# Expert outputs gated on leaving PSUM, split in two fp32r parts and summed by a 0/1 matrix, with w1 and w3 in separate blocks of 8 KB

## The chip, the cores and the metric

The kernel runs on one core of a Trainium2 chip. The metric is the device time of the whole kernel in microseconds (us), as the median of a few runs. The engines are named as in the profile: PE is TensorE's matrix product (PEld its weight load), DVE is VectorE, ACT is ScalarE, POOL is GpSimd, SP is SyncE, which here mostly issues DMAs.

## The reference, cut to what matters

Two transformer blocks run one after the other on 1024 tokens of 1024 numbers. The change touches only the mixture of experts of the first. It has 64 experts in 8 groups of 8. A token takes one group and in it two experts. Each expert is three matrices, w1 and w3 of 1024 x 256 and w2 of 256 x 1024, so 1 MiB each in fp32.

```python
g_sel = jnp.argmax(g_logits, axis=-1)
g_w = g_prob[tok, g_sel]
...
top_p, top_i = lax.top_k(e_prob, MOE_TOPK)
gates = g_w[:, None] * top_p / jnp.sum(top_p, axis=-1, keepdims=True)
expert_id = g_sel[:, None] * MOE_PER_GROUP + top_i
...
    hid = jax.nn.silu(xb @ w1[e]) * (xb @ w3[e])
    return hid @ w2[e]
...
ys = ys * slot_gate[:, None].astype(ys.dtype)
out = jnp.zeros((n_tok + 1, dm), ys.dtype).at[slot_tok].add(ys)[:n_tok]
```

## The kernel before

The program is three phases: a gated linear attention block, the mixture of experts (`phase_moe`), and the second block. `phase_moe` keeps the tokens of a group together, at most 160 rows a group, and works on **pairs of experts**: 32 iterations (p = 0 to 31), four pairs to a group, each expert with 64 slots for its rows. The two experts of a pair share TensorE's array: one writes the PSUM rows 0 to 63, the other 64 to 127.

*One iteration on TensorE, in order.* `down_t` turns the hidden values of pair p-1 (two transposes into `mhd`, copied by VectorE to `hidT`, L1002). `slots_in` gathers the rows of pair p into slots, 32 bf16 products by a 0/1 matrix `Ms` (L1189, L1194), copied by ScalarE to `xT`. `rows_out(p - 2)` adds the outputs `my` of pair p-2 into the group's rows: a product by `MwT`, which holds each slot's gate at its token, of two halves of 512 columns for the first 128 tokens (L1220, into `Y0`) and of four quarters of 256 columns side by side for the other 32 (L1224, into `Y1`); each result leaves PSUM by an addition on VectorE, or by a copy for the first pair of a group (L1214, L1216). `hidden(p)` is eight contraction steps for two experts, w1 and w3 side by side as 512 columns (L986), fp32 in two passes; then ScalarE's silu (L990) and VectorE's product (L992). `turned` turns the gate matrix `Mw` of the pair to `MwT` (two transposes into `mwt`, one copy on ScalarE, L1205). `down(p - 1)` multiplies by w2 in two halves (L1014), the first copied to `my` by ScalarE, the second by VectorE (both L1016). `masks(p + 1)` builds the next `Ms` and `Mw` on VectorE (L1177 to L1180) ahead of that copy.

*PSUM.* The outputs of `down` and of `rows_out` share three buffers called `mpy`; `mh`, `mhd` and `mwt` have one each.

*The loads.* All weights of the experts are read on SP's queue in the order of the program: `load_13` (L918 to L925) reads w1 and w3 of an expert into columns 0 to 255 and 256 to 511 of one tile of 128 x 8 x 512, so each row of eight steps lands in pieces of 256 numbers, 1 KB; `load_2` (L926 to L928) reads w2 in pieces of 8 KB. There are seven slots (`Slots`): iteration p issues w1 and w3 of experts 2p+7 and 2p+8 (from p = 12 on one fewer ahead) and w2 of two experts. The DMAs carry their completions on eight semaphore lanes, used in turn by SP's loads and by ScalarE's stores of a group's rows (`y_d`, `write_group`, L1161 to L1166, after every fourth pair); a DMA waits for the last one on its lane.

Of the kernel before, what the change touches and what calls it, by code (L numbers as in the profile page):

```python
# [8 lines left out]
F32 = mybir.dt.float32  # L9
F32R = mybir.dt.float32r  # L10
# [3 lines left out]
ACT = mybir.ActivationFunctionType  # L14
ALU = mybir.AluOpType
# [55 lines left out]
class Slots:  # L71
# [24 lines left out]
    def w13(self, i):  # L96

        if i == 1:
            return self.raw.rearrange("p a (b c) -> p (a b) c", c=512)
        return self.tile(i, "w13", [128, 8, 512])  # L100

    def w2(self, i):
        return self.tile(i, "w2", [128, 2, D])
# [809 lines left out]
def expert_loads(k, w1, w3, w2):  # L913

    nc = k.nc

    def row(w, e):
        return w[e] if isinstance(e, int) else w[bass.ds(e, 1)].rearrange("o a b -> (o a) b")  # L918

    def load_13(e, w, parts=1, eng=(nc.sync, nc.sync)):  # L920
        n = 8 // parts
        for k0 in range(0, 8, n):
            for c, src in enumerate((w1, w3)):
                eng[c].dma_start(out=w[:, k0:k0 + n, c * 256:c * 256 + 256],  # L924
                                 in_=row(src, e).rearrange("(p k) f -> p k f", k=8)[:, k0:k0 + n, :])  # L925

    def load_2(e, w, eng=nc.sync):
        eng.dma_start(out=w, in_=row(w2, e).rearrange("(p k) d -> p k d", k=2))  # L928

    return load_13, load_2  # L930


def phase_moe(k, h2_d, x1_d, y_d, keep, slots, load_13, load_2, w0):

    tc, nc = k.tc, k.nc
    V, S, G = nc.vector, nc.scalar, nc.gpsimd
    with ExitStack() as ctx:
# [22 lines left out]

        get_2(1)

        for name, n in (("my", D), ("MwT", GCAP)):
            sp.tile([128, n], F32, name=name)
        xa, xb = slots.xg, sp.tile([64, D], F32, name="xg1")
        i128 = sp.tile([128, 128], F32, name="mi128")
        G.iota(i128, pattern=[[1, 128]], base=0, channel_multiplier=0, allow_small_or_imprecise_dtypes=True)
# [12 lines left out]
        def hidden(xT, *ws):  # L980

            n = 64 * len(ws)
            h = php.tile([128, 512], F32, name="mh", tag="mh")
            for kk in range(8):
                for c, w in enumerate(ws):
                    nc.tensor.matmul(h[c * 64:c * 64 + 64, :], xT[:, kk, c * 64:c * 64 + 64], w[:, kk, :],  # L986
                                     start=(kk == 0), stop=(kk == 7), skip_group_check=True)

            hid = sp.tile([128, 2, 128], F32, name="hid")
            S.activation(out=hid[0:n].rearrange("s k p -> s p k"), in_=h[0:n, 0:256].rearrange("s (p k) -> s p k", k=2),  # L990
                         func=ACT.Silu)
# [12 lines left out]

        def down(hT, *ws):

            n = 64 * len(ws)
            y = sp.tile([128, D], F32, name="my")
            for half, copy in ((0, S.copy), (1, V.tensor_copy)):
                cs = slice(half * 512, half * 512 + 512)  # L1010
                ps = pyp.tile([128, 512], F32, name="mpy", tag="mpy")
                for kk in range(2):
                    for c, w in enumerate(ws):
                        nc.tensor.matmul(ps[c * 64:c * 64 + 64, :], hT[:, kk, c * 64:c * 64 + 64], w[:, kk, cs],  # L1014
                                         start=(kk == 0), stop=(kk == 1), skip_group_check=True)
# [17 lines left out]
        with tc.If(most > GCAP), ExitStack() as over:  # L1033
# [83 lines left out]

            V.tensor_scalar(out=ox, in0=og[:, 0:NB], scalar1=float(FAR), scalar2=None, op0=ALU.add)
            wa, wb = slots.w13(6), slots.w2(6)
            x = ov.tile([64, D], F32, name="ox")  # L1120
            V.memset(x, 0.0)
            for j in range(NB):
                e = nc.sync.value_load(ebi[0:1, j:j + 1], min_val=0, max_val=63)
                load_13(e, wa)
                load_2(e, wb)
                gather(x, h2_d, ox[0:64, j:j + 1])
                xT = sp.tile([128, 8, 128], F32, name="xT")
                for half in range(2):
                    ps = ptp.tile([128, 4, 128], F32, name="mtr", tag="mtr")
                    for i in range(4):  # L1130
                        kk = half * 4 + i
                        k.transpose(ps[:, i, 0:64], x[:, kk * 128:(kk + 1) * 128])
                    S.copy(out=xT[:, half * 4:half * 4 + 4, 0:64], in_=ps[:, :, 0:64])
                y = list(down(down_t(hidden(xT, wa)), wb))[-1]
# [11 lines left out]
        Y0, Y1 = yp.tile([128, D], F32, name="Y0"), yp.tile([128, 256], F32, name="Y1")  # L1146

        def parts(eng=G, cuts=(slice(0, D),)):

# [12 lines left out]
        def write_group(g):  # L1162
            r = g * GCAP
            for cs in (slice(0, D),) if g < 7 else (slice(0, 512), slice(512, D)):
                S.dma_start(out=y_d[r:r + 128, cs], in_=Y0[:, cs])
            S.dma_start(out=y_d[r + 128:r + GCAP, :].rearrange("t (h c) -> h t c", h=4), in_=Y1)  # L1166

        def masks(p):

# [29 lines left out]
        def turned(w):  # L1199

            ps = phd.tile([128, GCAP], F32, name="mwt", tag="mwt")
            k.transpose(ps[:, 0:128], w[:, 0, :])
            k.transpose(ps[:, 128:GCAP], w[0:32, 1, :])
            wT = sp.tile([128, GCAP], F32, name="MwT", bufs=2)
            S.copy(out=wT, in_=ps)  # L1205
            return wT

        def rows_out(p, wT, y):

            first = p % 4 == 0  # L1210

            def into(out, ps, copy):
                if first:
                    copy(out, ps)  # L1214
                else:
                    V.tensor_tensor(out=out, in0=ps, in1=out, op=ALU.add)  # L1216
            for half in range(2):
                cs = slice(half * 512, half * 512 + 512)
                ps = pyp.tile([128, 512], F32, name="mpy", tag="mpy")
                nc.tensor.matmul(ps, wT[:, 0:128], y[:, cs], start=True, stop=True)  # L1220
                into(Y0[:, cs], ps, (S.copy, V.tensor_copy)[half])
            ps = pyp.tile([128, 256], F32, name="mpy1", tag="mpy")
# [15 lines left out]
        def pair(d, q):  # L1238
            return d.pop(2 * q), d.pop(2 * q + 1)
# [3 lines left out]
        for p in range(NP):  # L1243
            if p:
                hT = down_t(hid)
            xT = slots_in(m[0])
            if p > 1:
                rows_out(p - 2, wT.pop(p - 2), ys.pop(p - 2))
# [12 lines left out]
            if p:  # L1261
                d = down(hT, *pair(w2, p - 1))
# [1387 lines left out]
```

## Time and profile before

| | |
|---|---|
| median of three runs | 2372.03 us (2367.10 to 2373.81) |
| profiled execution | 2370.45 us |
| its span in the profile | 2368.5 us, granted clock 0.973 on the mean |
| PE busy over the span | 2235.8 us, 94% |
| DVE, ACT, POOL busy | 1376.2, 859.9, 569.1 us |
| bytes moved by DMA | 408.61 MB, 173 GB/s on the mean |

The profiled execution is one of its own, and the page's times lie within its span. An engine's busy time is a sum over stages that have different limits. The loop over pairs is the stretch from about 570 to 1080 us; read the rows below for that stretch and not for the whole.

### The profile page before, as it was taken

To read this page: it belongs to the slowest core of one execution; us is meant where nothing else is said; L and a number is where in the kernel's file an instruction comes from. 1 tells how busy PE (TensorE), PEld (TensorE's weight loads), DVE (VectorE), ACT (ScalarE), POOL (GpSimd) and SP (SyncE) were. 2 spreads that over 40 slices of the span, in tenths; PEclk is the share of its full clock that TensorE was granted. 3 is DMA by queue.
4 is the path that set the end of the run, shared out by engine and by line. 5 is a ranking of instruction groups with operands and counts; after the bars stand their busy time and mean duration, and the time that the engine had idled before them with its cause. 6 is when DMAs were issued, how large, how long until landed. Compare 5 with 4: busy or idle time off the path is not lost.

```text
span 2368.5 us, 31053 instructions
## 1 busy us (share of the span) xinstructions
PE 2235.8 (94%) x11879; PEld 1609.8 (68%) x11879; DVE 1376.2 (58%) x2378; ACT 859.9 (36%) x1610; POOL 569.1 (24%) x520
## 2 busy tenths in 40 slices
PE   8899999996999999998999999999979999999996
PEld 7778888873444444434766788777768888887884
DVE  4766524564443333325355524666588888878988
ACT  4342434311222222214443334424444444444443
POOL 3222223201111111005300100346443333310036
PEclk9999999996999999997999999999989999999999
DMA  5544211648999999997511022444432222227442
GB/s 175 180 123 140 90 33 31 241 179 302 382 395 384 378 374 397 389 395 209 144 39 30 10 43 58 147 99 134 160 98 81 81 81 84 84 91 293 132 138 80
DMA packets 325054, 408.61 MB, mean 173 GB/s; under 512 B 43016, under 2 KB 264312, under 8 KB 316704
## 3 DMA queue, kind: packets, MB, share of 16 engines
q1 hardware_dynamic: 312064, 368.23, 45.9%
q0 software_dynamic: 4944, 18.37, 2.7%
q10 hardware_dynamic: 7888, 19.93, 2.2%
q8 instruction: 96, 1.57, 0.3%
q14 instruction: 62, 0.51, 0.1%
HBM read 360.29 MB, written 46.19 MB: 172 GB/s over the span
## 4 chain that ended last, share of the span: by engine, by line
PE 57%; DVE 5%; DMA 5%; SPq 3%; issue 3%; POOL 2%; ACT 2%; POOLq 0%; DVEq 0%; ACTq 0%
PE mh L986 8%; PE pu L2208 5%; PE pu L2211 5%; PE pu L2210 5%; PE mpy L1014 4%; PE pj L1356 2%; PE pj L1354 2%; PE pj L1352 2%; SPq L924 2%; PE pu L2389 2%; PE mpy L1220 2%; PE pu L2390 2%; PE pu L2387 2%; DMA w<-in_moe_w_dram 2%; PE mtr L1189 1%
## 5 line engine op out<-in xcount | busy, mean ns | idle before, releaser
L986 PE MATMUL mh<-w,xT 128*64 128x512 f32 x880 | 233.4, 598 | 5.7 <-DMA w<-in_moe_w_dram 5.1
L136 POOL TENSOR_TENSOR whl<-wraw,whl 128x1024 fp32r<-128x1024 f32 x35 | 87.1, 2494 | 327.7 <-ACT whl L135 186.5
L986 PEld LDWEIGHTS mh<-w,xT 128*64 128x64 f32 x880 | 76.0, 137 | 123.7 <-issue 108.9
L992 DVE TENSOR_TENSOR hid<-hid,mh 128x256 f32<-128x256 f32 x32 | 13.5, 421 | 220.5 <-ACT hid L990 220.5
L1014 PE MATMUL mpy<-w,hidT 128*64 128x512 f32 x512 | 117.1, 599 | 0.0
L1159 POOL TENSOR_TENSOR xg<-xg,xp 32x1024 f32<-32x1024 f32 x7 | 20.3, 2904 | 372.1 <-ACT xp L1155 372.1
L309 PE MATMUL pj<-hT,whl 128*128 128x512 f32 x256 | 105.4, 412 | 0.7 <-ACT rT L447 0.7
L1356 PE MATMUL pj<-hT,whl 128*128 128x512 f32 x256 | 102.9, 402 | 0.5 <-POOL whl L136 0.5
L1354 PE MATMUL pj<-hT,whl 128*128 128x512 f32 x256 | 103.0, 402 | 0.0
L1352 PE MATMUL pj<-hT,whl 128*128 128x512 f32 x256 | 102.3, 400 | 0.0
L990 ACT ACTIVATE hid<-mh 128x256 f32<-128x256 f32 x32 | 19.8, 619 | 223.9 <-PE mh L986 223.9
L311 PE MATMUL pj<-hT,whl 128*128 128x512 f32 x256 | 100.7, 394 | 0.0
L310 PE MATMUL pj<-hT,whl 128*128 128x512 f32 x256 | 100.5, 393 | 0.0
L2096 POOL TENSOR_TENSOR gr<-wraw,gr 128x512 f32<-128x512 f32 x30 | 58.0, 1932 | 164.2 <-DVE wup L136 59.1
L258 PE MATMUL pj<-whl,hT 128*128 128x256 f32 x256 | 82.5, 322 | 0.6 <-ACT hT L135 0.4
L2217 DVE TENSOR_TENSOR fup<-pu,fup 128x512 f32<-128x512 f32 x100 | 68.6, 686 | 23.0 <-PE pu L2211 23.0
L2389 PE MATMUL pu<-wup 128*128 128x512 f32 x180 | 71.7, 398 | 6.6 <-DVE wup L136 6.6
L259 PE MATMUL pj<-whl,hT 128*128 128x256 f32 x256 | 74.5, 291 | 2.0 <-POOL whl L136 2.0
L260 PE MATMUL pj<-whl,hT 128*128 128x256 f32 x256 | 74.3, 290 | 0.0
L1014 PEld LDWEIGHTS mpy<-w,hidT 128*64 128x64 f32 x512 | 33.8, 136 | 56.1 <-issue 49.1
L504 DVE SCALAR_TENSOR_TENSOR oT<-oT,cv 128x512 f32<-128x512 f32 x84 | 70.5, 839 | 1.4
L2390 PE MATMUL pu<-wup 128*128 128x512 f32 x180 | 70.6, 392 | 0.0
(742 smaller groups left out, 6414.3 us busy)
## 6 DMA issues: line engine op xcount, KB each, us to landing
w<-in_moe_w_dram SPq DMA_DIRECT2D x164, 1024.0 KB
oT<-in_w_ada_dram SPq DMA_DIRECT2D x96, 256.0 KB
wraw<-in_w_up_dram SPq DMA_DIRECT2D x34, 512.0 KB
wraw<-in_moe_w_dram SPq DMA_DIRECT2D x16, 1024.0 KB
wraw<-in_gla_w_in_dram SPq DMA_DIRECT2D x24, 512.0 KB
wraw<-in_w_in_dram SPq DMA_DIRECT2D x22, 512.0 KB
act_d<-act SPq DMA_DIRECT2D x22, 512.0 KB
wraw<-in_w_down_dram SPq DMA_DIRECT2D x42, 256.0 KB
```

The lines of the kernel that those rows point to most:

```text
L309: nc.tensor.matmul(ps, w[:, 0, cs], hT[:, 0, kk, sl], start=(kk == 0), stop=False)
L311: nc.tensor.matmul(ps, w[:, 1, cs], hT[:, 0, kk, sl], start=False, stop=(kk == 7))
L986: nc.tensor.matmul(h[c * 64:c * 64 + 64, :], xT[:, kk, c * 64:c * 64 + 64], w[:, kk, :], start=(kk == 0), stop=(kk == 7), skip_group_check ...
L1014: nc.tensor.matmul(ps[c * 64:c * 64 + 64, :], hT[:, kk, c * 64:c * 64 + 64], w[:, kk, cs], start=(kk == 0), stop=(kk == 1), skip_group_che ...
L1352: nc.tensor.matmul(ps, w[:, 0, cs], hT[:, 0, kk, sl], start=(kk == 0), stop=False)
L1354: nc.tensor.matmul(ps, w[:, 0, cs], hT[:, 1, kk, sl], start=False, stop=False)
L1356: nc.tensor.matmul(ps, w[:, 1, cs], hT[:, 0, kk, sl], start=False, stop=(kk == 7))
L2208: nc.tensor.matmul(ps, w[:, 0, cs], hi[:, kk, :], start=(kk == 0 and q in (1, 6, 7, 5)), stop=False, skip_group_check=True)
L2210: nc.tensor.matmul(ps, w[:, 0, cs], lo[:, kk, :], start=False, stop=False, skip_group_check=True)
L2211: nc.tensor.matmul(ps, w[:, 1, cs], hi[:, kk, :], start=False, stop=(kk == 3), skip_group_check=True)
L2389: nc.tensor.matmul(ps, a[:, 0, ts], w[:, 1, :], start=False, stop=False, skip_group_check=True)
L2390: nc.tensor.matmul(ps, a[:, 1, ts], w[:, 0, :], start=False, stop=(kk == 10), skip_group_check=True)
```

## The change

Four things are edited, and the rest follows from them.

1. w1 and w3 go into two blocks of the tile (`w13` is now 128 x 2 x 8 x 256), so a row of one expert's matrix lands as one piece of 8 KB. `hidden` reads its 512 columns as two runs of 256, one from each block.
2. The gates move from the sum to the outputs: `turned` makes `MwT` a 0/1 matrix by a comparison on VectorE, and ScalarE sums its rows to `Mgate`, one gate per slot. `down` scales by it on leaving PSUM.
3. `my` has two fp32r parts: ScalarE writes the scaled output rounded, VectorE the scaled output less that. `rows_out` multiplies both by the 0/1 matrix and adds them in PSUM, with 512 columns each; `Y1` is 32 x 1024 now.
4. The software DMA queue's scratch is halved (8192 bytes).

Blocks beyond a group's 160 rows or an expert's 64 go through a branch of their own, which keeps plain copies (`down1`).

```diff
-        return self.tile(i, "w13", [128, 8, 512])
+        return self.tile(i, "w13", [128, 2, 8, 256])
...
-                eng[c].dma_start(out=w[:, k0:k0 + n, c * 256:c * 256 + 256],
+                eng[c].dma_start(out=w[:, c, k0:k0 + n, :],
...
-                    nc.tensor.matmul(h[c * 64:c * 64 + 64, :], xT[:, kk, c * 64:c * 64 + 64], w[:, kk, :],
-                                     start=(kk == 0), stop=(kk == 7), skip_group_check=True)
+                    nc.tensor.matmul(h[c * 64:c * 64 + 64, :].rearrange("s (a f) -> s a f", a=2),
+                                     xT[:, kk, c * 64:c * 64 + 64], w[:, :, kk, :], start=(kk == 0), stop=(kk == 7),
+                                     skip_group_check=True)
...
-        def down(hT, *ws):
+        def down(hT, gate, *ws):
...
-            y = sp.tile([128, D], F32, name="my")
-            for half, copy in ((0, S.copy), (1, V.tensor_copy)):
+            y = sp.tile([128, 2, D], F32R, name="my")
+            for half in range(2):
...
-                copy(y[0:n, cs], ps[0:n])
+                S.activation(out=y[0:n, 0, cs], in_=ps[0:n], func=ACT.Copy, scale=gate)
+                V.scalar_tensor_tensor(out=y[0:n, 1, cs], in0=ps[0:n], scalar=gate, in1=y[0:n, 0, cs].bitcast(F32),
+                                       op0=ALU.mult, op1=ALU.subtract)
...
-            wT = sp.tile([128, GCAP], F32, name="MwT", bufs=2)
-            S.copy(out=wT, in_=ps)
-            return wT
+            wT = sp.tile([128, GCAP], F32R, name="MwT", bufs=2)
+            gate = sp.tile([128, 1], F32, name="Mgate", bufs=2)
+            junk = sp.tile([128, GCAP], F32, name="Mj")
+            V.tensor_scalar(out=wT, in0=ps, scalar1=0.0, scalar2=None, op0=ALU.not_equal)
+            S.activation(out=junk, in_=ps, func=ACT.Copy, accum_out=gate)
+            return wT, gate
...
-            for half in range(2):
-                cs = slice(half * 512, half * 512 + 512)
-                ps = pyp.tile([128, 512], F32, name="mpy", tag="mpy")
-                nc.tensor.matmul(ps, wT[:, 0:128], y[:, cs], start=True, stop=True)
-                into(Y0[:, cs], ps, (S.copy, V.tensor_copy)[half])
-            ps = pyp.tile([128, 256], F32, name="mpy1", tag="mpy")
-            for i in range(4):
-                nc.tensor.matmul(ps[i * 32:i * 32 + 32], wT[:, 128:GCAP], y[:, i * 256:i * 256 + 256], start=True,
-                                 stop=True, skip_group_check=True)
-            into(Y1, ps, S.copy)
+            for Yn, n, r in ((Y0, 128, 0), (Y1, GCAP - 128, 128)):
+                for half in range(2):
+                    cs = slice(half * 512, half * 512 + 512)
+                    ps = pyp.tile([128, 512], F32, name="mpy", tag="mpy")[0:n]
+                    for i in range(2):
+                        nc.tensor.matmul(ps, wT[:, r:r + n], y[:, i, cs], start=(i == 0), stop=(i == 1))
+                    into(Yn[:, cs], ps, (S.copy, V.tensor_copy)[half])
...
-    nc = _bacc.Bacc("TRN2", target_bir_lowering=False, num_devices=1)
+    nc = _bacc.Bacc("TRN2", target_bir_lowering=False, num_devices=1, dynamic_dma_scratch_size=8192)
```

On TensorE, between the gathering of a pair's slots (L1194) and its hidden product (L986), there stood before:

```order
L1194 LDWEIGHTS xp_9277
L1194 MATMUL mtr<-Ms,xp_9277 128x128
L1220 MATMUL mpy<-my,MwT 128x512 x2
L1224 MATMUL mpy_10802<-my,MwT 32x256 x4
L986 MATMUL mh<-w_5_4720,xT 64x512
L986 MATMUL mh<-w_6_5046,xT 64x512
```

And in the changed program, at the same place of another pair:

```order
L1209 LDWEIGHTS xp_9276
L1209 MATMUL mtr<-Ms,xp_9276 128x128
L1240 MATMUL mpy<-my,MwT 128x512 x4
L1240 MATMUL mpy<-my,MwT 32x512 x4
L986 MATMUL mh<-wraw,xT 64x512
L986 MATMUL mh<-w_3_4708,xT 64x512
```

The sum is eight products in place of six, at the same place; what stands around it has not moved.

On VectorE, from the second half of a pair's masks (L1177) to the next pair's hidden product (L992), there stood before:

```order
L1177 TENSOR_SCALAR Ma<-mi_4703,cq 128x128 [waits DVE_49]
L1178 SCALAR_TENSOR_TENSOR Ms<-mi_4703,cq,Ma 128x128 [waits DVE_49]
L1179 TENSOR_SCALAR Mw<-mi_4703,cq,sgate 128x128
L1180 SCALAR_TENSOR_TENSOR Mw<-Ma,sgate,Mw 128x128 [waits DVE_49]
L1016 COPY my<-mpy 128x512 [waits PE_49]
L1002 COPY hidT<-mhd 128x256 [waits PE_49]
L1216 TENSOR_TENSOR Y_9278<-mpy,Y_9278 128x512 [waits PE_49] x2
L1216 TENSOR_TENSOR Y_9279<-mpy_10349,Y_9279 128x256 [waits PE_49]
L992 TENSOR_TENSOR hid<-hid,mh 128x256 [waits Activation_49]
```

And in the changed program, up to the comparison that now follows the hidden product (L1222):

```order
L1192 TENSOR_SCALAR Ma<-mi_4703,cq 128x128 [waits DVE_49]
L1193 SCALAR_TENSOR_TENSOR Ms<-mi_4703,cq,Ma 128x128 [waits DVE_49]
L1194 TENSOR_SCALAR Mw<-mi_4703,cq,sgate 128x128
L1195 SCALAR_TENSOR_TENSOR Mw<-Ma,sgate,Mw 128x128 [waits DVE_49]
L1018 SCALAR_TENSOR_TENSOR my<-mpy,Mgate,my 128x512 [waits Activation_49] x2
L1003 COPY hidT<-mhd 128x256 [waits PE_49]
L1234 TENSOR_TENSOR Y_9277<-mpy,Y_9277 128x512 [waits PE_49] x2
L1234 TENSOR_TENSOR Y_9278<-mpy,Y_9278 32x512 [waits PE_49] x2
L993 TENSOR_TENSOR hid<-hid,mh 128x256 [waits Activation_49]
L1222 TENSOR_SCALAR MwT<-mwt 128x160 [waits PE_49]
```

Two passes that wait for ScalarE stand where one copy waited for TensorE, and the comparison stands ahead of the next masks.

## Rows read from the trace of the kernel before

**Rows 1.** Windows: stretch; us; PE, PEld, DVE, ACT, POOL busy; PEclk; DMA share; GB/s

```profile
720.00:760.00 40.00, 40.00 (x256) 16.62 (x255) 15.30 (x33) 10.93 (x18) 6.96 (x4) 1.00 1.07 398
960.00:1000.00 40.00, 37.53 (x218) 17.80 (x216) 13.20 (x28) 9.86 (x16) 3.76 (x2) 1.00 1.05 393
```

**Rows 2.** Timeline of ScalarE: start us; us; instruction; idle before and its releaser

```profile
606.58 0.62 ACT L990 ACTIVATE hid<-mh 128x256 f32<-128x256 f32 x1 [6.65 <-PE mh L986]
...
839.67 0.62 ACT L990 ACTIVATE hid<-mh 128x256 f32<-128x256 f32 x1 [8.55 <-PE mh L986]
...
1067.31 0.62 ACT L990 ACTIVATE hid<-mh 128x256 f32<-128x256 f32 x1 [8.46 <-PE mh L986]
```

**Rows 3.** Waits, 560 to 1085 us: who waited for what; us, times, longest

```profile
PE mh L986 <- DMA w<-in_moe_w_dram: 5.1, 3, 2.5
...
PEld mh L986 <- DMA w<-in_moe_w_dram: 4.4, 2, 2.6
```

**Rows 4.** Waits of SP's queue, the same stretch and columns

```profile
SPq L928 <- DMA y_d<-Y: 10.4, 3, 9.1
```

**Rows 5.** Timeline of SP's queue, 839 to 841 us

```profile
839.44 1.41 SPq L928 DMA_DIRECT2D w<-in_moe_w_dram  x2
```

**Rows 6.** Windows, around pair 17's silu, columns as in rows 1

```profile
837.50:840.50 3.00, 3.00 (x16) 1.02 (x14) 0.18 (x1) 0.76 (x2) 0.00 (x0) 1.00 0.47 131
```

**Rows 7.** DMA packets: 732 to 736 us (w1, w3), then 857.3 to 861.3 (w2)

```profile
DMA packets 1539, 1.54 MB, mean 386 GB/s; under 512 B 32, under 2 KB 1539, under 8 KB 1539
...
DMA packets 235, 1.71 MB, mean 428 GB/s; under 512 B 20, under 2 KB 28, under 8 KB 28
```

**Rows 8.** Timeline of PE, one pair's sums and its hidden product

```profile
798.95 1.94 PE L1220 MATMUL mpy<-my,MwT 128*128 128x512 f32 x4
...
801.38 0.64 PE L986 MATMUL mh<-wraw,xT 128*64 128x512 f32 x1
...
807.87 0.59 PE L986 MATMUL mh<-wraw,xT 128*64 128x512 f32 x1
```

**Rows 9.** Timeline of PE, fp32r products of the attention phase

```profile
250.06 0.39 PE L309 MATMUL pj<-hT,whl 128*128 128x512 f32 x1
...
250.74 0.39 PE L309 MATMUL pj<-hT,whl 128*128 128x512 f32 x1
...
48.02 0.39 PE L327 MATMUL pj<-hT,walr 128*32 128x512 f32 x1
48.24 0.40 PE L326 MATMUL pj<-hT,walr 128*32 128x512 f32 x1
...
41.64 0.28 PE L260 MATMUL pj<-whl,hT 128*128 128x256 f32 x1
41.76 0.28 PE L258 MATMUL pj<-whl,hT 128*128 128x256 f32 x1
```

**Rows 10.** Groups by line and shape (count; busy us, mean ns; idle before)

```profile
L1016 DVE COPY my<-mpy 128x512 f32<-128x512 f32 x32 | 22.1, 691 | 13.5 <-PE mpy L1014 13.5
L1016 ACT COPY my<-mpy 128x512 f32<-128x512 f32 x32 | 18.7, 585 | 54.7 <-PE mpy L1014 30.9 <-issue 14.1 <-DVE Mw L1180 9.6
L1216 DVE TENSOR_TENSOR Y<-mpy,Y 128x512 f32<-128x512 f32 x48 | 33.2, 692 | 49.1 <-PE mpy L1220 49.1
L1002 DVE COPY hidT<-mhd 128x256 f32<-128x256 f32 x32 | 13.3, 415 | 3.5 <-PE mpy L1014 3.5
L1205 ACT COPY MwT<-mwt 128x160 f32<-128x160 f32 x32 | 10.7, 333 | 0.0
...
L1750 DVE SCALAR_TENSOR_TENSOR xbcT<-u,cw,xbcT 128x512 f32<-128x512 f32 x39 | 28.7, 804 | 0.0
```

**Rows 11.** Timeline of VectorE, the end of one pair's masks

```profile
796.31 0.35 DVE L1180 SCALAR_TENSOR_TENSOR Mw<-Ma,sgate,Mw 128x128 f32<-128x128 bf16 x1
797.03 0.69 DVE L1016 COPY my<-mpy 128x512 f32<-128x512 f32 x1 [0.37 <-PE mpy L1014]
```

More of the change, by code (lines that the diff above doesn't have):

```diff
@@ L98, in w13 @@
         if i == 1:
-            return self.raw.rearrange("p a (b c) -> p (a b) c", c=512)
-        return self.tile(i, "w13", [128, 8, 512])
+            return self.raw.rearrange("p (c x) (b f) -> p c (x b) f", c=2, f=256)
+        return self.tile(i, "w13", [128, 2, 8, 256])
     def w2(self, i):
@@ L961, in phase_moe @@
         get_2(1)
-        for name, n in (("my", D), ("MwT", GCAP)):
-            sp.tile([128, n], F32, name=name)
+        sp.tile([128, 2, D], F32R, name="my")
+        sp.tile([128, GCAP], F32R, name="MwT")
         xa, xb = slots.xg, sp.tile([64, D], F32, name="xg1")
@@ L1015, in down, with down1 @@
                                          start=(kk == 0), stop=(kk == 1), skip_group_check=True)
-                copy(y[0:n, cs], ps[0:n])
+                S.activation(out=y[0:n, 0, cs], in_=ps[0:n], func=ACT.Copy, scale=gate)
+                V.scalar_tensor_tensor(out=y[0:n, 1, cs], in0=ps[0:n], scalar=gate, in1=y[0:n, 0, cs].bitcast(F32),
+                                       op0=ALU.mult, op1=ALU.subtract)
                 yield y[0:n]
+        def down1(hT, w):
+            y = sp.tile([128, 2, D], F32R, name="my").rearrange("p a d -> p (a d)").bitcast(F32)[0:64, 0:D]
+            for half, copy in ((0, S.copy), (1, V.tensor_copy)):
+                cs = slice(half * 512, half * 512 + 512)
+                ps = pyp.tile([128, 512], F32, name="mpy", tag="mpy")
+                for kk in range(2):
+                    nc.tensor.matmul(ps[0:64, :], hT[:, kk, 0:64], w[:, kk, cs], start=(kk == 0), stop=(kk == 1),
+                                     skip_group_check=True)
+                copy(y[:, cs], ps[0:64])
+            return y
         NP = 32
@@ L1119, in phase_moe @@
             wa, wb = slots.w13(6), slots.w2(6)
-            x = ov.tile([64, D], F32, name="ox")
+            x = xb
             V.memset(x, 0.0)
@@ L1133, in phase_moe @@
                     S.copy(out=xT[:, half * 4:half * 4 + 4, 0:64], in_=ps[:, :, 0:64])
-                y = list(down(down_t(hidden(xT, wa)), wb))[-1]
+                y = down1(down_t(hidden(xT, wa)), wb)
                 xo = sp.tile([128, 8, 128], F32, name="oxa", tag="xT")[0:64].rearrange("p a b -> p (a b)")
@@ L1145, in phase_moe @@
         pb = yp.tile([96, D], BF16, name="xp1")
-        Y0, Y1 = yp.tile([128, D], F32, name="Y0"), yp.tile([128, 256], F32, name="Y1")
+        Y0, Y1 = yp.tile([128, D], F32, name="Y0"), yp.tile([GCAP - 128, D], F32, name="Y1")
         def parts(eng=G, cuts=(slice(0, D),)):
@@ L1165, in write_group @@
                 S.dma_start(out=y_d[r:r + 128, cs], in_=Y0[:, cs])
-            S.dma_start(out=y_d[r + 128:r + GCAP, :].rearrange("t (h c) -> h t c", h=4), in_=Y1)
+            S.dma_start(out=y_d[r + 128:r + GCAP, :], in_=Y1)
         def masks(p):
@@ L1216, in into @@
                     V.tensor_tensor(out=out, in0=ps, in1=out, op=ALU.add)
-            for half in range(2):
-                cs = slice(half * 512, half * 512 + 512)
-                ps = pyp.tile([128, 512], F32, name="mpy", tag="mpy")
-                nc.tensor.matmul(ps, wT[:, 0:128], y[:, cs], start=True, stop=True)
-                into(Y0[:, cs], ps, (S.copy, V.tensor_copy)[half])
-            ps = pyp.tile([128, 256], F32, name="mpy1", tag="mpy")
-            for i in range(4):
-                nc.tensor.matmul(ps[i * 32:i * 32 + 32], wT[:, 128:GCAP], y[:, i * 256:i * 256 + 256], start=True,
-                                 stop=True, skip_group_check=True)
-            into(Y1, ps, S.copy)
+            for Yn, n, r in ((Y0, 128, 0), (Y1, GCAP - 128, 128)):
+                for half in range(2):
+                    cs = slice(half * 512, half * 512 + 512)
+                    ps = pyp.tile([128, 512], F32, name="mpy", tag="mpy")[0:n]
+                    for i in range(2):
+                        nc.tensor.matmul(ps, wT[:, r:r + n], y[:, i, cs], start=(i == 0), stop=(i == 1))
+                    into(Yn[:, cs], ps, (S.copy, V.tensor_copy)[half])
             if p % 4 == 3:
@@ L1247, in phase_moe @@
             if p > 1:
-                rows_out(p - 2, wT.pop(p - 2), ys.pop(p - 2))
+                rows_out(p - 2, wT.pop(p - 2)[0], ys.pop(p - 2))
             if p % 4 == 3 and p // 4 + 1 < 8:
@@ L1261, in phase_moe @@
             if p:
-                d = down(hT, *pair(w2, p - 1))
+                d = down(hT, wT[p - 1][1], *pair(w2, p - 1))
                 ys[p - 1] = next(d)
@@ L1268, in phase_moe @@
                 get_2(*range(*e2[-2:]))
-        rows_out(NP - 2, wT.pop(NP - 2), ys.pop(NP - 2))
-        y = list(down(hT, *pair(w2, NP - 1)))[-1]
-        rows_out(NP - 1, wT.pop(NP - 1), y)
+        rows_out(NP - 2, wT.pop(NP - 2)[0], ys.pop(NP - 2))
+        rows, gate = wT.pop(NP - 1)
+        y = list(down(hT, gate, *pair(w2, NP - 1)))[-1]
+        rows_out(NP - 1, rows, y)
 def pipeline(make, n, every=1, front=False):
```

## The prediction

> **What bounds the kernel now.** I read the busy time by stretch first, because the change lies in one stage: the expert loop, from about 570 to 1080 us of 2368.5. There TensorE is busy for the whole of 720 to 760 us, and the DMA engines are at a share above 1 in the same stretch [rows 1]. Two resources are full at once, so the question is which of them sets each part of the stage.
>
> The silu that follows each pair's first product (L990) marks the pairs. From pair 2 to pair 17 it comes every (839.67 - 606.58) / 15 = 15.54 us, from pair 17 to pair 31 every (1067.31 - 839.67) / 14 = 16.26 us [rows 2]. The first part has TensorE without a gap: TensorE binds. In the second, TensorE falls to 37.53 of 40 us [rows 1] and it waits for weights, 5.1 + 4.4 us by name [rows 3]. The excess over the first pace is 227.64 - 14 x 15.54 = 10.1 us. So the weight loads bind the second part.
>
> Why only there? SP's queue issues the loads in order, and each also waits for the last transfer on its semaphore lane, on which group outputs (y_d) ride too. SP stood 9.1 us in one such wait [rows 4]. It ended at 839.44 us [rows 5], beside pair 17's silu, while the DMA engines ran at a share of 0.47 [rows 6]. Counted along the queue, the load that was held back is w2 of expert 34; w1 and w3 of experts 38 to 63 come behind it, 52 transfers of 1 MiB (1,048,576 bytes). This wait ties the queue to TensorE's pace at pair 17, and wipes out whatever lead the queue had. I call it the gate.
>
> **The change part by part.** *Loads of w1 and w3.* Before, a row of an expert's matrix lands as eight runs of 1 KB; now as one of 8 KB. The bytes, their number of transfers and the waits on SP stay. In a stretch of the one kind (1539 packets, all under 2 KB) the rate is 386 GB/s; in one of w2, which already lands in 8 KB runs (207 of the 235 packets are not under 8 KB), it is 428 GB/s [rows 7]. One transfer takes 1.0486 MB / 386 = 2.717 us now, and / 428 = 2.450 us then: 0.267 us less.
>
> The Trainium skill, "DMA: Bandwidth & Descriptors", section Bandwidth, puts a fixed cost of about 3 cycles on each packet beside one cycle per 32 bytes, and says that joining packets is worth it only up to 256 bytes, which speaks against this part. By its figures 1 KB would cost 35 cycles and 8 KB 259, an estimate of 7.5% less time and 10.6 us over the 52 transfers, for a sum of 2355 us. The rows of this case show 9.8%, and they decide.
>
> *TensorE, output sums.* Now two fp32 products of 512 columns, each in two passes, and then four of 256 columns side by side: from the first at 798.95 to the next hidden product at 801.38, 2.43 us a pair [rows 8]. After, eight fp32r products of 512 columns, four of them with a 32-column stationary part. In the attention phase three of those, a triple of hi and lo products, take 250.74 - 250.06 = 0.68 us, 0.227 each, and with 32 columns the next starts after 0.22 [rows 9]. Eight take 1.82 us. I add 0.08 for entering and 0.05 for the third PSUM buffer: 1.95 us, 0.48 us less. Bounds: 0.61 less if nothing is added; none if the waits below eat it.
>
> *TensorE, hidden product.* Same count, but its moving operand is now two runs of 256 that lie 8 KB apart. No row has such an operand. From below: nothing, since the columns are the same. From above, by two separate products of 256 columns: they start 0.12 us apart [rows 9], so two take 0.24 for 0.227, and for the sixteen steps of a pair 0.2 us, or 0.4 if the two-pass form doubles it. I take nothing, the nearer reading for one instruction over the same columns, and keep 0.4 for the range.
>
> *VectorE and ScalarE.* A pair loses a 0.691 us copy on VectorE and gains two scalar-tensor-tensor passes (nearest: 0.804, at least the 0.691 of the copy), one comparison of 160 columns (at most the 0.333 of the copy that it replaces) and, in the sum, two evictions of 512 columns (0.692 each) in place of one of 256 [rows 10]. That is roughly 2.2 us more of a 15 us pair, in which VectorE works 15.30 of 40 us [rows 1]. ScalarE gains one 0.585 us eviction per pair. Work as such is covered; what counts is order. VectorE's masks end at 796.31 + 0.35, and its copy of y's second half now starts at 797.03 [rows 11]. Pushed by the comparison to about 797.0, the two passes end at 798.4 to 798.6, and hidT's copy (0.415) at about 799.0. The first sum is wanted from 798.95, its low part of the second half as fourth product at about 799.6, and the first eviction at about 799.6: covered by some 0.5 us. The fourth output buffer in turn is wanted 1.36 us after the first product, and the first is free after its two products and an eviction, 0.227 + 0.39 + 0.69 = 1.31 us, and what lies between them: that is the 0.05.
>
> *The tail.* After the last pair's down product nothing covers the chain: ScalarE's copy and then VectorE's pass in place of one copy (+0.7), eight products for six (-0.48), and one more eviction at the end (+0.7): I take 1.0 us more. Halving the software queue's scratch I cost at nothing: its gathers in the loop go out one group ahead of their use. No row gives a price if that cover goes.
>
> **The sum, against the profiled 2370.45 us.** Pairs 2 to 17 go at TensorE's pace: 15 x 0.48 = 7.2 us. From the gate on: the loads take 52 x 0.267 = 13.9 us less, 227.64 - 13.9 = 213.7 us; TensorE at 15.06 a pair would want 210.8. The loads still end last, so 13.9 us is what comes off, and TensorE keeps some 3 us of waits for weights. Less the tail: 7.2 + 13.9 - 1.0 = 20.1 us, 2350.3 us for that execution. The median of the runs is 1.6 us above it, so **2352 us**. Its own range goes by the bounds above. With 0.61 us for the sums and no tail it is 9.2 + 13.9 = 23.1 us, 2349; with 0.4 us for the hidden product, 0.08 a pair is left, the loads are no longer last, and it is 15 x 0.08 + 14 x 0.08 + 10.1 - 1.0 = 11.4 us, 2361.
>
> **The rivals.**
> *The loads keep up* (chance 0.20). If the DMA engines lose less elsewhere than I assume, TensorE binds throughout: 29 x 0.48 + 10.1 - 1.0 = 23.0 us, 2349. For it: 3 us of 214 decide. Against: the gate returns every fourth pair. With 0.61 instead of 0.48 it is 26.8 us and 2345, the low end.
> *The split holds TensorE up* (0.10). If the chain ScalarE, VectorE, fp32r part comes late by the 0.5 us that cover it, TensorE keeps its pace and only the waits for weights go: 10.1 - 1.0 = 9.1 us, 2363. For it: seven VectorE passes stand in a row where four stood. Against: 15.30 of 40 us busy.
> *Bigger packets load no faster* (0.12). If the 428 GB/s of w2 is a burst between slower loads and not a rate that holds, only the first 7.2 us come off, less the tail and about 1 us, since the loads now fall behind before the gate: 2367. The same section of the Trainium skill sets about 358 GB/s as the memory's limit for such a core, by which nothing would be gained; the stretches at 386 and 428 lie above that. Against: both rates stand side by side, with nothing else changed than the packet.
> *Slower: the two-run operand* (0.08). TensorE's hidden product is sixteen steps a pair, (807.87 - 801.38) / 15 = 0.43 us each [rows 8]. The gains at TensorE's pace are 0.48 a pair and 10.1 us once; they are gone when a pair's hidden product grows by 0.79 us, 0.05 a step, and at 0.065 a step the kernel is 0.3% slower. If a second run cost as much as a second instruction, every step would double: 29 x (6.9 - 0.48) - 9.1 = 177 us, 2549. For it: no row excludes it. Against: products of 256 columns take just over half the time of those of 512 [rows 9], so streaming and not the start of a run is what costs.
> That the change doesn't do what it says is no case: the loads stand in the built program as 128 x 2048, and the sums as fp32r products of 512 columns.
>
> **How the numbers follow.** The forecast has 0.50. A measurement of this kernel can tell about 0.3%, 7 us, from no change: faster is below 2364.9. That holds for the forecast, the keeping up and the late split: 0.80. Within 0.3%: the unhelped loads, 0.12. Slower: 0.08. The range of 2345 to 2366 takes in the forecast, the loads that keep up down to their low end, and the late split with 3 us for the hidden product's bound; left out are the slower rival and the unhelped loads, 0.20 together.
>
> **What would show it.** Right: w1 and w3 as 8 KB packets and near 428 GB/s in all stretches of the loop; pairs at about 15.06 us up to the gate, the silu of pair 17 about 7 us earlier; two to four us of waits for weights left, all behind pair 17; sums of about 1.95 us. Wrong: a step of hidden products above 0.43 us; a share of the DMA engines below 1 outside the y_d waits together with waits for weights; or TensorE waiting for y's second part on VectorE. A saving outside the loop would be no part of this.

## The result, and the profile after

The changed kernel takes **2351.6 us** (median of four runs, 2350.01 to 2353.68) against 2371.76 for the kernel before in the same comparison: a ratio of **0.9918, 95% interval 0.9901 to 0.9935**. The forecast was 2352.0. Its profiled execution took 2353.68 us, with a span of 2351.9. One run of the kernel with 2 KB pieces below took 4284.47 us, far out of line with all others, and is left out of its median.

The silu marks the pairs again. Timeline of ScalarE in the changed kernel (start us, us, instruction, idle before it and its releaser):

```profile
605.48 0.62 ACT L991 ACTIVATE hid<-mh 128x256 f32<-128x256 f32 x1 [7.24 <-PE mh L986]
...
833.17 0.62 ACT L991 ACTIVATE hid<-mh 128x256 f32<-128x256 f32 x1 [8.15 <-PE mh L986]
...
1046.13 0.62 ACT L991 ACTIVATE hid<-mh 128x256 f32<-128x256 f32 x1 [8.12 <-PE mh L986]
```

Against [rows 2], pairs 2 to 17 take 227.69 us in place of 233.09, so 15.18 a pair in place of 15.54: **5.4 us**. Pairs 17 to 31 take 212.96 in place of 227.64: **14.7 us**. The forecast had 7.2 and 13.9. So the loop gives 20.1 us. From profile to profile 1.1 us more come off ahead of pair 2 (605.48 for 606.58) and 4.6 are lost behind pair 31 (1305.8 for 1301.2), so the span is 16.6 us shorter. What the 4.6 are worth is asked below, with the scratch.

The same two stretches as in [rows 1], as windows (stretch; us; PE, PEld, DVE, ACT, POOL busy; PEclk; DMA share; GB/s):

```profile
720.00:760.00 40.00, 40.00 (x230) 16.33 (x228) 20.30 (x44) 12.52 (x22) 7.30 (x4) 1.00 1.01 422
960.00:1000.00 40.00, 39.96 (x242) 17.14 (x239) 19.71 (x40) 13.15 (x22) 5.59 (x3) 1.00 1.01 426
```

TensorE is full in both now, and the loads run at 422 and 426 GB/s. No wait of TensorE for weights is left [against rows 3]: the group of hidden products has 0.6 us of idle time, and ScalarE ends it. That is the row of the page; under it, from the waits of SP's queue (us, times, longest), what answers to [rows 4]:

```profile
L986 PE MATMUL mh<-w,xT 128*64 128x512 f32 x880 | 229.1, 598 | 0.6 <-ACT xT L1211 0.5
```

```profile
SPq L928 <- DMA y_d<-Y: 61.8, 8, 16.4
...
SPq L924 <- DMA y_d<-Y: 37.0, 3, 21.0
```

The kernel before had a second such row beside the 10.4 us of [rows 4]:

```profile
SPq L924 <- DMA y_d<-Y: 21.9, 4, 11.0
```

SP waits three times as long for the group stores as before, 98.8 us for 32.3, and TensorE waits for none of it. The length of a queue's wait doesn't say what it costs.

The packets of w1 and w3 at the place of the first of [rows 7], 732 to 736 us:

```profile
DMA packets 239, 1.70 MB, mean 426 GB/s; under 512 B 31, under 2 KB 31, under 8 KB 31
```

And one pair's sums up to the last hidden product, on TensorE, as in [rows 8]:

```profile
732.85 2.14 PE L1240 MATMUL mpy<-my,MwT 128*128 128x512 f32 x8
734.92 0.64 PE L986 MATMUL mh<-w,xT 128*64 128x512 f32 x1
...
741.41 0.59 PE L986 MATMUL mh<-w,xT 128*64 128x512 f32 x1
```

The sums take 734.92 - 732.85 = 2.07 us, not 1.95. The fifteen steps of the hidden product take 6.49 us, 0.433 each, as before: its two-run operand costs nothing. The same view of the kernel with a fourth output buffer, which comes below, has 2.02 us:

```profile
732.01 2.10 PE L1240 MATMUL mpy<-my,MwT 128*128 128x512 f32 x8
734.03 0.64 PE L986 MATMUL mh<-w,xT 128*64 128x512 f32 x1
```

### The profile page after: what moved, and what is told of

Its sections match the earlier page's. It is cut to its first block, busy times and chain, and to the rows that moved or that the text cites. A ratio compares the mean times of both kernels' runs of the same rounds, so it can differ in the third digit from the quotient of the medians.

```text
span 2351.9 us, 30956 instructions
## 1 busy us (share of the span) xinstructions
PE 2225.8 (95%) x11751; PEld 1612.3 (69%) x11751; DVE 1432.6 (61%) x2474; ACT 894.0 (38%) x1674; POOL 573.0 (24%) x520
## 4 chain that ended last, share of the span: by engine, by line
PE 61%; DVE 5%; DMA 3%; issue 3%; ACT 2%; POOL 2%; SPq 0%; POOLq 0%; ACTq 0%; DVEq 0%; another core or an unknown queue 0%
PE mh L986 9%; PE pu L2224 5%; PE pu L2227 5%; PE pu L2226 5%; PE mpy L1015 5%; PE mpy L1240 2%; PE pj L1372 2%; PE pj L1370 2%; PE pj L1368 2%; PE pu L2405 2%; PE pu L2406 2%; PE pu L2403 2%; PE mtr L1204 2%; PE ctr L1611 1%; PE ctr L131 1%
## 5 line engine op out<-in xcount | busy, mean ns | idle before, releaser
L986 PE MATMUL mh<-w,xT 128*64 128x512 f32 x880 | 229.1, 598 | 0.6 <-ACT xT L1211 0.5
L986 PEld LDWEIGHTS mh<-w,xT 128*64 128x64 f32 x880 | 71.4, 137 | 120.2 <-issue 117.3
L2405 PE MATMUL pu<-wup 128*128 128x512 f32 x180 | 71.7, 398 | 6.4 <-DVE wup L136 6.4
L1240 PE MATMUL mpy<-my,MwT 128*128 128x512 f32 (+1 forms) x256 | 70.6, 408 | 1.5 <-DVE my L1018 0.6
```

The costliest lines, as they stand in the source:

```text
L986: nc.tensor.matmul(h[c * 64:c * 64 + 64, :].rearrange("s (a f) -> s a f", a=2), xT[:, kk, c * 64:c * 64 + 64], w[:, :, kk, :], start=(kk = ...
L1240: nc.tensor.matmul(ps, wT[:, r:r + n], y[:, i, cs], start=(i == 0), stop=(i == 1))
L2405: nc.tensor.matmul(ps, a[:, 0, ts], w[:, 1, :], start=False, stop=False, skip_group_check=True)
```

## The experiments

**The two halves apart.** First the loads alone, in the kernel before.

```diff
+        return self.tile(i, "w13", [128, 2, 8, 256])
...
+                eng[c].dma_start(out=w[:, c, k0:k0 + n, :],
...
+                                     xT[:, kk, c * 64:c * 64 + 64], w[:, :, kk, :], start=(kk == 0), stop=(kk == 7),
```

> The kernel before with the load part of the change alone: w1 and w3 in two blocks of the tile, 8 KB pieces, the hidden product reading two runs; sums as before. Theory (each part has its own gain): TensorE keeps its 15.54 us a pair, since the sums are the old ones, and the loads end early enough that the 9.5 us of waits for weights go: pairs 2 to 31 take 29 x 15.54 = 450.7 in place of 460.7 us, so 10 us less, 2361.8. Rival 1 (the two-run operand costs something and the changed kernel hid it): steps of the hidden product above 0.433 us, so less than 10 us gained. Rival 2 (packets don't matter, the changed kernel's loads were quicker because they started otherwise): waits for weights of 5 us and more stay, 2367 to 2372.

Measured: 2359.59 us, ratio 0.9947 (0.9931 to 0.9962). Timeline of ScalarE:

```profile
605.59 0.62 ACT L991 ACTIVATE hid<-mh 128x256 f32<-128x256 f32 x1 [6.65 <-PE mh L986]
...
838.68 0.62 ACT L991 ACTIVATE hid<-mh 128x256 f32<-128x256 f32 x1 [8.55 <-PE mh L986]
...
1056.06 0.62 ACT L991 ACTIVATE hid<-mh 128x256 f32<-128x256 f32 x1 [8.46 <-PE mh L986]
```

Pairs 2 to 17 take 233.09 us, to the hundredth what they took before, and pairs 17 to 31 217.38, TensorE's pace. No row of a wait of TensorE for weights is left. The first theory holds: TensorE binds the first part, the loads bound the second, and the operand in two runs is free.

Then the changed kernel with the old loads.

```diff
-        return self.tile(i, "w13", [128, 2, 8, 256])
+        return self.tile(i, "w13", [128, 8, 512])
...
-                eng[c].dma_start(out=w[:, c, k0:k0 + n, :],
+                eng[c].dma_start(out=w[:, k0:k0 + n, c * 256:c * 256 + 256],
```

> The kernel before with the rest of the change and the old loads in 1 KB pieces: gates on leaving PSUM, two fp32r parts, eight products, halved scratch. Theory (the wait for the group stores ties the loads to TensorE at pair 17): 15 pairs gain 0.36 us each, 5.4 us, from there on the loads take 227.6 us as before; with 0.7 us lost at the end of the loop it is 4.7 us less, 2367, and waits for weights grow from 9.5 to about 15 us. Rival 1 (the parts add up: 29 x 0.36 less 0.7): 9.7 us less, 2362, with waits as before. Rival 2 (the loads' total binds from the start, nothing ties them): no gain, 2371 to 2373, waits near 20 us.

Measured: 2366.74 us, 0.9981 (0.9971 to 0.9990). Timeline of ScalarE, then the waits of TensorE for weights:

```profile
604.78 0.63 ACT L990 ACTIVATE hid<-mh 128x256 f32<-128x256 f32 x1 [7.22 <-PE mh L986]
...
832.47 0.62 ACT L990 ACTIVATE hid<-mh 128x256 f32<-128x256 f32 x1 [8.15 <-PE mh L986]
...
1062.04 0.62 ACT L990 ACTIVATE hid<-mh 128x256 f32<-128x256 f32 x1 [8.12 <-PE mh L986]
```

```profile
PE mh L986 <- DMA w<-in_moe_w_dram: 5.4, 6, 1.5
PEld mh L986 <- DMA w<-in_moe_w_dram: 5.2, 4, 2.4
...
PE mh L986 <- DMA wraw<-in_moe_w_dram: 1.2, 1, 1.2
```

The faster sums gain their 5.4 us up to pair 17, and then pairs 17 to 31 take 229.57 us, 1.9 more than before: TensorE catches up with the loads sooner and waits longer, 11.8 us in place of 9.5 (about 15 were expected). By themselves the sums bring 4.6 us and the loads 11.7, together 20.2. In the loop it is 3.5, 10.3 and 20.1: the parts don't add up, since the sums gain behind pair 17 only once the loads are faster.

**The scratch alone.**

```diff
-    nc = _bacc.Bacc("TRN2", target_bir_lowering=False, num_devices=1)
+    nc = _bacc.Bacc("TRN2", target_bir_lowering=False, num_devices=1, dynamic_dma_scratch_size=8192)
```

> The kernel before with the software queue's scratch halved and nothing else. Theory: nothing, within 0.1% of the kernel before, 2370 to 2374. Rival (the second block, which took 1286.5 us from the last group store to the end before and 1290.4 in the changed kernel's profile, pays for the smaller scratch): 1 to 4 us more, 2373 to 2376, and the same stretch near 1290 us.

Measured: 2371.74 us, 1.0002 (0.9993 to 1.0011): nothing. The stretch from pair 31's silu to the end took 1304.1 us here, 1301.2 in the kernel before and 1305.8 in the changed one, whose profiled execution was the slowest of its four. In the other kernels whose last stores ScalarE issues it lies between 1299.7 and 1304.9, and in those of them that have the sums of the change between 1300.9 and 1304.9. So the 4.6 us in that one profile are not shown to be the change's.

**How near the loads are.** The low parts' four products are taken out; the low parts are made and not added.

```diff
-                    for i in range(2):
-                        nc.tensor.matmul(ps, wT[:, r:r + n], y[:, i, cs], start=(i == 0), stop=(i == 1))
+                    nc.tensor.matmul(ps, wT[:, r:r + n], y[:, 0, cs], start=True, stop=True)
```

> The changed kernel without the four products of the low parts in each pair's sum: the low parts are still made on VectorE and then not added, so that work is left out. It takes 4 x 0.23 = 0.92 us of TensorE from each pair. Theory (the loads of the changed kernel keep up by about 1 us only: the least slack between the landing of a w1 or w3 and its use is 0.9 us): TensorE would need 26.7 us less over 29 pairs, but the loads give it some 1 to 4 us, so 2348 to 2351, and waits for weights of 20 us or more come back. Rival (TensorE alone sets the pace and the loads follow it, since they wait for its slots): 24 to 27 us less, 2325 to 2328, with hardly a wait for weights.

Measured: 2344.08 us, 0.9890 (0.9873 to 0.9908): less than the first theory's 2348, and far from the rival's 2328. The theory left out that TensorE gains freely up to pair 17: 6.2 us come off there and 0.3 behind. Two things held the kernel up. Pairs 2 to 17 take 14.76 us each, a gain of 0.41 for 0.92 us of products. One pair's sums on TensorE show why:

```profile
803.34 0.94 PE L1239 MATMUL mpy<-my,MwT 128*128 128x512 f32 x3
804.60 0.42 PE L1239 MATMUL mpy<-my,MwT 128*32 128x512 f32 x1 [0.32 <-DVE Y L1234]
804.95 1.51 PE L986 MATMUL mh<-w,xT 128*64 128x512 f32 x6
```

The fourth output waits for an eviction on VectorE, as there are three buffers. The timeline of ScalarE shows the other:

```profile
826.85 0.62 ACT L991 ACTIVATE hid<-mh 128x256 f32<-128x256 f32 x1 [7.70 <-PE mh L986]
...
1039.47 0.62 ACT L991 ACTIVATE hid<-mh 128x256 f32<-128x256 f32 x1 [7.66 <-PE mh L986]
```

Pairs 17 to 31 take 212.62 us where TensorE alone would want 14 x 14.76 = 206.7, and waits for weights are back:

```profile
PEld mh L986 <- DMA w<-in_moe_w_dram: 2.4, 2, 1.5
...
PE mh L986 <- DMA w<-in_moe_w_dram: 0.6, 1, 0.6
```

That is 3.0 us by name and 5.9 by the pace; the 20 us that were expected were far too many. So the loads, store waits included, need about 212.6 us from pair 17 on here, and the changed kernel's TensorE takes 212.96. The two limits lie within about a microsecond of each other, as the least slack in the changed kernel's trace says: w1 and w3 of pair 30 land 0.9 us ahead of their use.

**The store wait.** In the kernel before, POOL's software queue issues the group stores, so SP's loads no longer share lanes with them.

```diff
-                S.dma_start(out=y_d[r:r + 128, cs], in_=Y0[:, cs])
+                G.dma_start(out=y_d[r:r + 128, cs], in_=Y0[:, cs])
```

> The kernel before with the group stores (y_d) issued by POOL's software queue in place of ScalarE's, so that they no longer ride on the eight lanes that SP's loads wait for; loads in 1 KB pieces and sums as before. Theory (the store wait on SP's queue, 32 us in sum, costs the loads their lead): the waits for weights go, pairs 2 to 31 take 29 x 15.54 = 450.7 us, so 10 us less than before, 2361. Rival (the DMA engines are full either way and SP's wait at the stores only stands in front of a full queue): pairs 17 to 31 stay at 227 us, waits for weights at 8 to 10 us, 2370 to 2372.

Measured: 2373.27 us, 1.0009 (0.9998 to 1.0020). By the time alone the rival wins, but the loop of the profiled execution did gain: pairs 17 to 31 took 221.09 us, 6.5 less. The stretch behind pair 31 took 1309.3 us, 8 more. Timeline of POOL and TensorE at the loop's end:

```profile
1076.71 0.73 POOL L1166 DMA_DIRECT2D y_d<-Y  x1
...
1077.63 0.51 POOL L1401 DMA_DIRECT2D rows<-in_final_norm_dram  x1
...
1081.53 3.75 PE L1394 MATMUL prow<-rows,ones 1*128 1x512 f32 x4 [5.83 <-DMA rows<-in_final_norm_dram]
```

The last group's stores stand on POOL ahead of the second block's preparation. In the kernel before, POOL issued that load at 1056.05 us, long before the loop's end. So the last group went back to ScalarE:

```diff
+                (G if g < 7 else S).dma_start(out=y_d[r:r + 128, cs], in_=Y0[:, cs])
```

> The kernel before with the stores of groups 0 to 6 issued by POOL's software queue and those of the last group by ScalarE as before. Theory (the stores by POOL gained 6.6 us in the loop and lost it behind it, because the second block's preparation stands behind the last group's stores on POOL): the loop's gain stays, pairs 2 to 31 at 454 us, and the loss goes, the stretch from pair 31's silu to the end at 1301 to 1304 us again, so 2365. Rival (software stores cost something everywhere): 2370 to 2373 again, with that stretch near 1309.

Measured: 2364.76 us, 0.9968 (0.9957 to 0.9980), on the first theory. Timeline of ScalarE:

```profile
839.20 0.61 ACT L990 ACTIVATE hid<-mh 128x256 f32<-128x256 f32 x1 [8.49 <-PE mh L986]
...
1059.57 0.62 ACT L990 ACTIVATE hid<-mh 128x256 f32<-128x256 f32 x1 [8.46 <-PE mh L986]
```

220.37 us for pairs 17 to 31, and 1299.7 behind. Of the 10.1 us that the loads cost the kernel before, 7.3 go when the store wait goes. What is left is 2.8 us over TensorE's 217.5. The 8 KB pieces take off all of it with the store waits still there, so the 10.1 us are not the work of one cause: either cure gives the loads most of the time that they lacked.

The same move, without the correction for the last group, in the kernel of the high parts:

> The kernel of the high parts alone (low parts made and not added) with the group stores issued by POOL's software queue. Theory (the store wait on SP's queue is what still ends last there): pairs 17 to 31 go from 212.6 to TensorE's 14 x 14.77 = 206.7 us, 5.9 us less, 2338, waits for weights gone. Rival (the DMA engines' rate is the limit): 212 us and 2344 as without it.

Measured: 2346.98 us, 0.9905 (0.9885 to 0.9926). Again the loop has it (207.41 us for pairs 17 to 31, TensorE's pace of 14.76 and 0.7 us in all), and the stretch behind gives it back, 1310.3 us. So the store wait is what held the loads at 212.62 in that kernel.

**The packet.** The changed kernel with w1 and w3 interleaved every two steps.

```diff
-        return self.tile(i, "w13", [128, 2, 8, 256])
+        return self.tile(i, "w13", [128, 4, 2, 2, 256])
```

> The changed kernel with w1 and w3 interleaved every two steps, so that they land in pieces of 2 KB in place of 8 KB; all else as in the changed kernel. Theory (each packet costs a fixed part, worked out from 1 KB at 386 and 8 KB at 428 GB/s: per engine 42.4 ns for 1 KB and 306 ns for 8 KB, so 37.7 ns a KB and 4.7 ns a packet): 2 KB at 40.1 ns a KB, 409 GB/s, one transfer 2.56 us; over the 52 transfers behind the store wait 5.7 us more than with 8 KB, of which the changed kernel has about 1 us of slack, so 4 to 5 us more, 2356, with a few us of waits for weights. Rival (the gain comes all at once at some size of piece): 428 GB/s and 2351.6, or 386 GB/s and 14 us more, 2365.

Measured: 2353.33 us (three runs, 2352.91 to 2356.66), 0.9924 (0.9904 to 0.9945), where 2356 was expected. The time rules out the 2365 of the rival, but its interval overlaps that of the change; the trace has to decide the rest. The packets, 732 to 736 us:

```profile
DMA packets 820, 1.64 MB, mean 409 GB/s; under 512 B 21, under 2 KB 21, under 8 KB 820
```

409 GB/s as expected, so a fixed cost per packet fits all three sizes. The waits for weights are back, 4.4 us, and in the profiled execution, the slowest of the three, pairs 17 to 31 take 217.98 us, 5.0 more than with 8 KB.

Could it be SP, which has to issue more pieces, in place of the DMA engines? In the kernel before it issued a w1 or w3 in 1 KB pieces in 0.55 us right behind the wait at pair 17, when the DMA engines ran at a share of 0.47 [rows 6]; a transfer takes 2.717 us. So issuing is not what limits the rate. Timeline of SP's queue in the kernel before:

```profile
840.90 0.55 SPq L924 DMA_DIRECT2D w<-in_moe_w_dram  x1
```

**The third buffer.**

```diff
-        pyp = pool("m_py", 3, space=PSUM)
+        pyp = pool("m_py", 4, space=PSUM)
...
-            ps = phd.tile([128, GCAP], F32, name="mwt", tag="mwt")
+            ps = phd.tile([128, 2, 128], F32, name="mwt", tag="mhd").rearrange("p a b -> p (a b)")[:, 0:GCAP]
```

> The changed kernel with a fourth output buffer in PSUM; the two small transposed tiles share one bank for it. Theory (the third buffer holds the sums up by what the trace shows: 0.02 us a pair, 0.19 in the first pair of a group, 0.47 once): 29 x 0.02 + 8 x 0.19 + 0.47 = 2.6 us less at most, sums of 2.05 us in every pair, 2349 to 2351. Rival (the shared bank makes the transposes wait for the evictions): pairs get longer, 2353 and more.

Measured: 2349.46 us, 0.9911 (0.9894 to 0.9927). Timeline of ScalarE:

```profile
605.41 0.62 ACT L991 ACTIVATE hid<-mh 128x256 f32<-128x256 f32 x1 [7.01 <-PE mh L986]
...
1043.26 0.64 ACT L991 ACTIVATE hid<-mh 128x256 f32<-128x256 f32 x1 [8.09 <-PE mh L986]
```

Pairs 2 to 31 take 437.85 us, 2.8 less than in the changed kernel, 2.6 expected. The sums take 2.01 to 2.03 us in every pair of the loop, so the third buffer had cost 0.05 in most pairs, more than the 0.02 expected, and 0.24 in the first pair of a group, of which the stretch has fewer than the expectation counted: the two errors offset each other.

> The changed kernel with the fourth output buffer and with the stores of groups 0 to 6 by POOL. Theory (with the fourth buffer TensorE has no wait left in the loop, so a lighter load queue gains nothing): as with the fourth buffer alone, pairs 2 to 31 at 438 us, 2348 to 2351. Rival (the loads' lead still ends in late pairs and every store wait counts): 3 us less, 2346.

Measured: 2348.76 us, 0.9902 (0.9888 to 0.9916), pairs 2 to 31 at 437.70: with TensorE full, the lighter queue gains nothing. It is the lowest time of a kernel that computes everything, but its interval overlaps that of the change.

**Both limits off.** High parts alone, four buffers, stores of groups 0 to 6 by POOL.

> High parts alone (the low parts are made and not added), with the fourth buffer, and the stores of groups 0 to 6 by POOL. Theory (the sums are held up by the fourth buffer and the loads by the store wait): a sum of four products takes 0.32 + 2 x 0.23 + 0.35 = 1.13 us in place of 1.61, pairs about 14.17 us, 29 of them 411 us, and the loads (six transfers of 2.45 us a pair, and stores and gathers of some 0.8 us) can follow only with the lead that they start with, so 411 to 416 us for pairs 2 to 31, 2322 to 2328. Rival (something else holds TensorE at 14.7 us): 427 us and more, 2338.

Measured: 2330.10 us, 0.9825 (0.9810 to 0.9841), above the 2322 to 2328 expected. Timeline of ScalarE, pairs 2, 21 and 31:

```profile
601.72 0.63 ACT L991 ACTIVATE hid<-mh 128x256 f32<-128x256 f32 x1 [6.25 <-PE mh L986]
...
871.01 0.62 ACT L991 ACTIVATE hid<-mh 128x256 f32<-128x256 f32 x1 [7.19 <-PE mh L986]
...
1024.66 0.62 ACT L991 ACTIVATE hid<-mh 128x256 f32<-128x256 f32 x1 [7.16 <-PE mh L986]
```

Up to pair 21 a pair takes 269.29 / 19 = 14.17 us, as worked out: the sums are priced right once the buffer is there. From then on it takes 153.65 / 10 = 15.37 us. That is the loads' own pace with 8 KB pieces and no store wait, at 425 GB/s on the mean. The expectation trusted the lead to last; it is spent at pair 21. The window, columns as in [rows 1]:

```profile
871.00:1024.00 153.00, 149.27 (x880) 66.36 (x879) 75.39 (x168) 45.60 (x84) 20.14 (x18) 1.00 1.01 425
```

## Why the prediction was right, and where its sum was not

The median fell on the forecast, 2351.6 for 2352.0. The profiled execution, for which the sum was made, did not: 2350.3 was forecast and 2353.68 measured. The steps one by one:

- *What bounds which part*: right. The loads alone left pairs 2 to 17 untouched and took all waits out behind. But the loads took over later than pair 17. In the kernel before, pair 21's silu stands here:

```profile
901.80 0.62 ACT L990 ACTIVATE hid<-mh 128x256 f32<-128x256 f32 x1 [8.55 <-PE mh L986]
```

Pairs 17 to 21 still came every (901.80 - 839.67) / 4 = 15.53 us, and all of the 10.1 us fall behind them.

- *The loads*: right. 426 GB/s against 428, so 2.46 us a transfer for 2.45. The 213.7 us for pairs 17 to 31 show as 212.6 in the run where the loads end last. The Trainium skill, "DMA: Bandwidth & Descriptors", section Bandwidth, holds joining packets worth it only up to 256 bytes; here 1, 2 and 8 KB load at 386, 409 and 426 GB/s. By the fixed cost that the Trainium skill gives there, 8 KB would take 7.5% less time than 1 KB, an estimate; 9.4% was measured.
- *The gate*: right that it costs: 7.3 of the 10.1 us went with it. It did not wipe out the whole lead, for w1 and w3 of pair 18 still landed 8 us ahead of their use. And it does not tie the loads for good: once they are faster, SP waits three times as long there and TensorE not at all, until TensorE is faster too, as with the high parts alone (212.62 us with the store wait, 207.41 without).
- *The sums*: the step that failed, "1.95 us, 0.48 us less". They take 2.07, 0.36 less. The starts of the eight products in the trace give it: the first takes 0.32 us to the next, six take 0.23 to 0.25, and from the last to the hidden product it is 0.33. The forecast had the entry (0.09 over the pace), but no exit (0.10 over the pace). Its 0.05 for the third buffer holds in most pairs; the first of a group takes 0.19 more, where an eviction on ScalarE comes late, and once it is 0.47. The kernel before pays a like price between fp32 products of different shapes:

```profile
800.29 0.59 PE L1220 MATMUL mpy<-my,MwT 128*128 128x512 f32 x1
800.81 0.64 PE L1224 MATMUL mpy<-my,MwT 128*32 128x256 f32 x8
```

From its last half to its first quarter it is 0.52 us, where the halves stand 0.43 apart. So a row of the kernel before could have priced the exit, and the price is not one of fp32r alone. What causes it is not shown. That the mean pair gains 0.36 too is in part chance: most go from 15.54 to 15.14, a little more than the sums alone give, and the first of a group only to 15.33.

- *The hidden product, the scratch*: nothing, as taken. The slower rival is out.
- *VectorE's cover*: held. TensorE's products waited 0.6 us for the low parts in the whole stage and its weight loads 1.2, all of it behind the loop, and the pass costs 0.748 us, within the bounds of 0.691 and 0.804.
- *The tail*: 1.0 us forecast. From pair 31's silu to the last store's issue it was 1081.45 - 1067.31 = 14.14 us before, and 1061.17 - 1046.13 = 15.04 now: 0.9.
- *Who ends last*: wrong. "The loads still end last" and "TensorE keeps some 3 us of waits for weights" rested on 210.8 us for TensorE. With 0.36 in place of 0.48 it is 212.96, and the loads' 212.6, read where TensorE is faster, stay just below. So the rival in which the loads keep up is what happened in kind, at 29 x 0.36 + 10.1 - 0.9 = 19.6 us instead of its 23.0.

By its own terms the gain is 5.4 + 14.7 - 0.9 = 19.2 us where 20.1 was forecast and the medians show 20.2. The sum was near since the error fell where two limits cross: 1.8 us too much up to pair 17, 0.8 too little behind it. That it came within half a microsecond is luck; that it came within a few is not, because where two limits lie within 3 us of 214, mistaking the one for the other costs no more than that.

Rows of the groups that were priced, in the changed kernel (count; busy us, mean ns; idle before), 560 to 1085 us:

```profile
L1018 DVE SCALAR_TENSOR_TENSOR my<-mpy,Mgate,my 128x512 fp32r<-128x512 f32 x64 | 47.8, 748 | 7.6 <-ACT my L1017 5.0
L1017 ACT ACTIVATE my<-mpy,Mgate 128x512 fp32r<-128x512 f32 x64 | 44.0, 687 | 50.6 <-PE mpy L1015 50.6
L1240 PE MATMUL mpy<-my,MwT 128*128 128x512 f32 x128 | 38.5, 417 | 0.8 <-DVE my L1018 0.6
...
L1222 DVE TENSOR_SCALAR MwT<-mwt 128x160 fp32r<-128x160 f32 x32 | 10.2, 317 | 0.0
```

The 0.6 us behind L1240 are what TensorE's products waited for the low parts. And the waits of its weight loads for a free output buffer (us, times, longest), which the fourth buffer removed:

```profile
PEld mpy L1240 <- DVE Y L1234: 8.3, 23, 0.4
...
PEld mpy L1240 <- ACT Y L1232: 4.7, 8, 0.8
```

## What to carry to other kernels

Price a faster part by the pace of the next limit as well as by its own: here each half of the change was worth 4.6 and 11.7 us alone and 20.2 together. Where one kind of product follows another, price the entry and the exit, not only the products, and count the buffers that the shorter products now wait for. When a queue is relieved by moving work to another, read what stands behind it there: the same stores cost 8 us behind the loop on POOL until the last group stayed where it was.

## What the runs showed of the hardware

- A packet cost 4.7 ns on an engine besides 37.7 ns a KB, worked out from 1 KB at 386 and 8 KB at 428 GB/s; it gave the 409 GB/s of 2 KB.
- A product whose moving operand is two runs of 256 columns, 8 KB apart, starts every 0.433 us, like one of a single run.
- Between fp32r products of 512 columns and other work there are some 0.09 us before and 0.10 after that a run of equal products doesn't show. Between fp32 products of 512 columns and of 256 side by side it was 0.09 too.
- ScalarE's scaled eviction of 128 x 512 to fp32r takes 0.687 us, where the plain copy took 0.585 [rows 10].
